# Decay matrices of the mLSTM: stabiliser rows by transposes of broadcast columns, the causal mask added by VectorE

## The chip, the cores and the metric

The kernel runs on one core of a Trainium2 chip. The metric is the device time of one execution in microseconds. A core has a tensor engine (PE, with its weight loads listed apart as PEld), a vector engine (DVE), a scalar engine (ACT), GpSimd (POOL) and SyncE (SP), which issues DMAs here. Each engine works through its own instruction queue in order and waits on semaphores for the others. TensorE writes to PSUM; VectorE and ScalarE read PSUM and SBUF.

## The reference, cut to what matters

The program is one step of a one-layer hybrid decoder: a half-step SwiGLU FFN, a mixer (mLSTM heads beside sliding-window attention heads, one input and one output projection), and a second half-step FFN, on a prompt of 1024 tokens and a batch of 8 x 4 sample tokens. The change lies in the mLSTM's chunk step:

```python
b = jnp.cumsum(jax.nn.log_sigmoid(fg), axis=-1)
causal = jnp.tril(jnp.ones((L, L), dtype=bool))
D = jnp.where(causal, b[..., :, None] - b[..., None, :] + ig[..., None, :], -jnp.inf)
inter = b + m[..., None]
m_t = jnp.maximum(inter, jnp.max(D, axis=-1))
W = jnp.exp(D - m_t[..., None])                 # the decay matrix
S = jnp.einsum('bhtd,bhsd->bhts', q, k) * W
num = a[..., None] * jnp.einsum('bhtk,bhkv->bhtv', q, C) + jnp.einsum('bhts,bhsv->bhtv', S, v)
```

With a_s = ig_s - b_s and M_t the running maximum, W is exp(a_s - M_t) for s <= t and 0 elsewhere. The kernel holds it transposed: s on the partitions, t along the row, four heads side by side. So a_s is a column (the bias of the exponential), -M_t is a row that has to stand on every partition, and the mask is a large negative number where s > t.

## The kernel before, in words

The prompt's mLSTM is cut into chunks 0 to 7 of 128 tokens; chunk 8 holds the 32 sample tokens. All projections are dense products in three single-precision passes (`mm3`, recorded at L163 as all products are); they fill nearly all of TensorE's queue. The work of the mLSTM, the attention and the gates is spawned as generator tasks of a planner (`Order`). The planner keeps a clock, `od.now`, which `pe()` (L157) advances for each product that is issued: 0.11 us for a transpose (`tr=True`, recorded at L160), for a plain fp32 product 4 x max(n, 64)/2400 us. When a task's due time comes, its next step is issued between two dense products. So the program's order on each engine is fixed at build time, and the planner's costs take part in it. The Tile layer then adds the waits.

`gates` (L1378) works on the four heads as 4 partitions: the row I holds -M_t at its end, and G the four groups of columns that the chunk step needs. One transpose of G per chunk (`gT`) and one VectorE copy give `K.cols[:, c]`: for each of the chunk's 128 tokens 4 groups x 4 heads. `gates_sample` (L1414) does the same for chunk 8.

`decay_matrix` (L1671) makes E = W for a chunk. In a PSUM bank named E (pool "a", two banks, shared with the scores S and the transposed keys tT) TensorE sums a product of a bf16 identity with the mask `maskb` (128 x 512) and four fp32 products of a one-hot column of the identity (4 partitions) with the rows H, which put -M_t on all partitions. ScalarE then takes four exponentials from PSUM to SBUF (L1682), each with its bias column. `scores` (L1685) makes S = k q on TensorE, and VectorE multiplies S into E (L1693). `state_keys` (L1697) transposes the keys (tT) and VectorE scales them (kw, L1705). `mlstm_state` then uses E (intra) and kw (U), `mlstm_norm` ends the chunk (hn, hT). `mlstm_sample` (L1802) calls `scores` for chunk 8 with slices of 32. The bf16 identity `identb` is made in `mix_setup` (L1294) from the fp32 one.

Around chunks 0 to 3 the dense work is the input projection (`po`, `pz`); around chunks 5 to 7 it is the rest of that and the output projection (`pw`), with the gating of the finished chunks (z, og, ul) on VectorE and ScalarE.

Of the kernel before, what the change touches and what calls it, by code (L numbers as in the profile page):

```python
# [9 lines left out]
F32 = mybir.dt.float32  # L10
F32R = mybir.dt.float32r
BF16 = mybir.dt.bfloat16
I32 = mybir.dt.int32
AF = mybir.ActivationFunctionType
ALU = mybir.AluOpType

P = 128
# [1231 lines left out]
HM = 4  # L1249
# [44 lines left out]
def mix_setup(K):  # L1294
    nc, A = K.nc, K.A
    mk = tmp(K, "mk", 162)
    nc.sync.dma_start(mk, A["c_mask"])
    K.maskb = K.cp.tile([P, 160], BF16, tag="maskb", name="maskb")
    nc.vector.tensor_copy(K.maskb, mk[:, 0:160])
    K.bmask = K.cp.tile([P, 2], F32, tag="bmask", name="bmask")  # L1300
    nc.vector.tensor_copy(K.bmask, mk[:, 160:162])
    K.identb = K.cp.tile([P, P], BF16, tag="identb", name="identb")
    nc.vector.tensor_copy(K.identb, K.ident)
    K.zero = K.cp.tile([P, 1], F32, tag="zero", name="zero")
    nc.vector.memset(K.zero, 0.0)
    K.bg = K.cp.tile([P, 8], F32, tag="bg", name="bg")
    nc.sync.dma_start(K.bg, A["b_gate"].to_broadcast([P, 8]))
    K.m0 = K.cp.tile([4, 8], F32, tag="m0", name="m0")
    nc.sync.dma_start(K.m0, A["state_mlstm_m"][0].rearrange("b h -> h b"))
    sk = K.cp.tile([8, 1], F32, tag="sk", name="sk")  # L1310
    nc.sync.dma_start(sk, A["attn_sinks"][0].rearrange("(h o) -> h o", o=1))
    ps = sbank(K, "sk")
    pe(K, ps[:, 0:8], sk.to_broadcast([8, P]), K.ident[0:8, 0:8], start=True, stop=True)
    oh = tmp(K, "oh", P)[0:8]
    nc.vector.tensor_copy(oh.rearrange("p (b h t) -> p b h t", b=4, h=8),
                          K.ident[0:8, 0:8].unsqueeze(1).unsqueeze(3).to_broadcast([8, 4, 8, 4]))
    pe(K, ps[:, 8:9], oh, sk, start=True, stop=True)
    K.sink = K.cp.tile([P, 9], F32, tag="sink", name="sink")
    nc.vector.tensor_copy(K.sink, ps[:, 0:9])
    K.cols = K.cp.tile([P, 9, 4, 4], F32, tag="cols", name="cols")  # L1320
    K.dec = K.cp.tile([P, 2, 4, 8], F32, tag="dec", name="dec")
    K.mst = K.cp.tile([4, 9], F32, tag="mst", name="mst")
    nc.vector.memset(K.mst[:, 0:1], 0.0)

    K.sz = K.cp.tile([P, 14, 32], F32, tag="sz", name="sz")
# [52 lines left out]
def gates(K, n):  # L1378

    nc = K.nc  # L1380
    I, lf = K.H[n]
    b, G = tmp2(K, "gb")[0:4], slot(K, "G")
    nc.gpsimd.memset(G, 0.0)
    chunks = [(c, loc(c)[1]) for c in range(4 * n, 4 * n + 4)]
    one = K.ones[0:4].to_broadcast([4, P])
    zero = K.zero[0:4].to_broadcast([4, P])
    a = G[0:4]
    for c, o in chunks:
        nc.vector.tensor_tensor_scan(b[:, o:o + P], one, lf[:, o:o + P], 0.0, ALU.mult, ALU.add)
    M, d = lf, b  # L1390
    p = lambda x: pair(x)[:, :, 0:2 * P]
    nc.vector.tensor_tensor(p(a), p(I), p(b), op=ALU.subtract)
    for c, o in chunks:
        nc.vector.tensor_tensor_scan(M[:, o:o + P], zero, a[:, o:o + P], K.mst[:, c:c + 1], ALU.add, ALU.max)
        nc.vector.tensor_tensor(K.mst[:, c + 1:c + 2], b[:, o + P - 1:o + P], M[:, o + P - 1:o + P], op=ALU.add)
    nc.vector.tensor_scalar(p(I), p(M), -1.0, None, op0=ALU.mult)
    nc.vector.tensor_tensor(p(d), p(b), p(M), op=ALU.add)
    yield 7.0
    nc.scalar.activation(p(G[64:68]), p(d), AF.Exp, scale=-1.0)
    for c, o in chunks:  # L1400
        nc.scalar.activation(G[32:36, o:o + P], M[:, o:o + P], AF.Exp, bias=K.mst[:, c:c + 1], scale=-1.0)
        nc.scalar.activation(G[96:100, o:o + P], a[:, o:o + P], AF.Exp, bias=I[:, o + P - 1:o + P])
    if n == 1:
        nc.sync.dma_start(K.O["p_m"][0, 0].rearrange("(h o) -> h o", o=1), K.mst[:, 8:9])
    yield 9.0
    dec_bcast(K, [G[32:36, o + P - 1:o + P] for c, o in chunks], 0, 4 * n)
    for c, o in chunks:
        ps = bank(K, "gT", "b")
        pe(K, ps[:, 0:100], G[0:100, o:o + P], K.ident[0:100, 0:100], tr=True)
        nc.vector.tensor_copy(K.cols[:, c], ps[:, 0:P].rearrange("p (y s) -> p y s", s=32)[:, :, 0:4])  # L1410
    K.od.done.add(("gates", n))


def gates_sample(K):  # L1414

    nc = K.nc
    I, b = K.H[2]
    M, w, d = [K.Hs[:, 64 + 32 * i:96 + 32 * i] for i in range(3)]
    G4 = tmp(K, "G", P)
    nc.gpsimd.memset(G4, 0.0)  # L1420
    G = G4[:, 0:32]
    a = G[0:4]
    v4 = lambda x: x.rearrange("p (b t) -> p b t", t=4)
    for s in range(1, 4):
        nc.vector.tensor_tensor(v4(b)[:, :, s], v4(b)[:, :, s], v4(b)[:, :, s - 1], op=ALU.add)
    nc.vector.tensor_tensor(a, I, b, op=ALU.subtract)
    for s in range(4):
        prev = K.m0 if s == 0 else v4(M)[:, :, s - 1]
        nc.vector.tensor_tensor(v4(M)[:, :, s], v4(a)[:, :, s], prev, op=ALU.max)
    nc.vector.tensor_tensor(d, b, M, op=ALU.add)  # L1430
    nc.scalar.activation(G[64:68], d, AF.Exp, scale=-1.0)
    nc.vector.tensor_tensor(v4(w), K.m0.unsqueeze(2).to_broadcast([4, 8, 4]), v4(M), op=ALU.subtract)
    nc.vector.tensor_tensor(v4(b), v4(a), v4(M)[:, :, 3:4].to_broadcast([4, 8, 4]), op=ALU.subtract)
    nc.vector.tensor_scalar(I, M, -1.0, None, op0=ALU.mult)
    nc.scalar.activation(G[32:36], w, AF.Exp)
    nc.scalar.activation(G[96:100], b, AF.Exp)
    mn = small(K, "mn", 8)[0:4]
    nc.vector.tensor_copy(mn, v4(d)[:, :, 3])
    nc.sync.dma_start(K.O["s_m"][0].rearrange("b h -> h b"), mn)
    yield 9.0  # L1440
    dec_bcast(K, [v4(G[32:36])[:, :, 3]], 1, 0)
    ps = bank(K, "gT", "b")
    nc.gpsimd.tensor_copy(G4[:, 32:P].rearrange("p (c t) -> p c t", c=3), G.unsqueeze(1).to_broadcast([P, 3, 32]))
    pe(K, ps[:, 0:100], G4[0:100], K.ident[0:100, 0:100], tr=True)
    nc.vector.tensor_copy(K.cols[:, 8], ps[:, 0:P].rearrange("p (y s) -> p y s", s=32)[:, :, 0:4])

    ps = bank(K, "scol", "b")
    for h in range(HM):
        pe(K, ps[32 * h:32 * h + 32, 0:4], G[0:100], K.ident[0:100, h::32],
           start=True, stop=True, tile_position=(0, 32 * h))  # L1450
    K.scc = K.cp.tile([P, 4], F32, tag="scc", name="scc")
    nc.vector.tensor_copy(K.scc, ps[:, 0:4])
    K.od.done.add(("gates", 2))
# [214 lines left out]
    return r  # L1668


def decay_matrix(K, H, c, w, home):  # L1671

    nc = K.nc
    ps = bank(K, "E", "a")
    mask = K.maskb[:, 0:P] if w == P else K.maskb[0:32, P:160]
    pe(K, ps[0:w, 0:4 * w].rearrange("p (h t) -> p h t", h=4), K.identb[0:w, 0:w],
       mask.unsqueeze(1).to_broadcast([w, 4, w]), start=True, stop=False)
    for h in range(HM):
        pe(K, ps[0:w, h * w:(h + 1) * w], K.ident[0:4, h:h + 1].to_broadcast([4, w]), H, start=False, stop=(h == HM - 1))
    E = home(K, "E")[:, 0:4 * w]  # L1680
    for h in range(HM):
        nc.scalar.activation(E[0:w, h * w:(h + 1) * w], ps[0:w, h * w:(h + 1) * w], AF.Exp,  # L1682
                             bias=K.cols[0:w, c, 0, h:h + 1])
    return E


def scores(K, c, k, q, H, w, home):

    E = decay_matrix(K, H, c, w, home)
    S = bank(K, "S", "a")  # L1690
    for h in range(HM):
        pe(K, S[0:w, h * w:(h + 1) * w], k[h], q[h], start=True, stop=True)
    K.nc.vector.tensor_tensor(E[0:w], S[0:w, 0:4 * w], E[0:w], op=ALU.mult)  # L1693
    return E

# [15 lines left out]
def chunk_scores(K, c):  # L1711
    n, o = loc(c)
    k = [K.k[h][n][:, o:o + P] for h in range(HM)]
    E = scores(K, c, k, [K.q[h][n][:, o:o + P] for h in range(HM)], K.H[n][0][:, o:o + P], P, tmp)
    return E, state_keys(K, k, [K.cols[:, c, 3, :]], tmp)[0]


# [84 lines left out]
def mlstm_sample(K):  # L1802

    nc, A, O = K.nc, K.A, K.O
    c = 8
# [10 lines left out]
    ps = bank(K, "n0T", "c")  # L1816
# [2 lines left out]
    nc.vector.tensor_copy(n0.rearrange("p b h -> p (b h)"), ps[:, 0:32])  # L1819
    for b in range(8):  # L1820
        state(b)
    E = scores(K, c, [K.sz[:, 6 + h] for h in range(HM)], [K.sz[:, 10 + h] for h in range(HM)], K.H[2][0], 32, slot)

    kr = slot(K, "kr")[:, 0:512]
    nc.gpsimd.tensor_copy(kr.rearrange("p (h c t) -> p h c t", h=4, c=4),
# [9 lines left out]
    for hp in range(2):  # L1835
        q = slot(K, "qm")[:, 0:512]
# [7 lines left out]
    for b0 in range(0, 8, 2):  # L1844
# [3 lines left out]
        for b, Cb in zip(bs, C):  # L1848
            for h in range(HM):
                q = qm[h // 2][:, (h % 2) * 256 + b * 32:(h % 2) * 256 + b * 32 + 32]  # L1850
                pe(K, pi[32 * h:32 * h + 32, 0:129], q, Cb[:, h], start=(b == 0), stop=(b == 7),
                   tile_position=(0, 32 * h))
        for hp in range(2):
            pu = [bank(K, "sU", "ba"[hp]) for b in bs]
            for x in range(2):
                h = 2 * hp + x
# [4 lines left out]
            for b, ps, Cb in zip(bs, pu, C):  # L1861
                for x in range(2):
                    h = 2 * hp + x
# [325 lines left out]
```

## Time and profile before

| | |
|---|---|
| median of three runs | 1987.2 us (1985.57 to 1987.73) |
| the profiled execution's own time | 1986.58 us |
| its span | 1984.8 us |
| TensorE busy | 1956.4 us, 99% |
| VectorE busy | 1229.6 us, 62% |
| ScalarE busy | 901.6 us, 45% |
| granted TensorE clock, mean | 0.999 of full speed |

The span is the time from the first to the last recorded instruction of the profiled execution; its own time is 1.8 us above. Busy shares are means over the whole span; the mLSTM's chunks lie between about 1007 and 1150 us of it. In a timeline a group of like instructions stands in one row with the start of the first and the time to the end of the last; matmuls overlap, so the step from one row's start to the next one's tells what a group takes of the engine.

### The profile page before, as it was taken

What the parts mean: (1) busy time and instruction counts of PE and PEld (TensorE: products, weight loads), DVE (VectorE), ACT (ScalarE), POOL (GpSimd) and SP (SyncE); (2) the same over time, 40 slices, a digit from 0 to 9 for tenths busy, and PEclk for the clock granted to TensorE, in tenths of its full rate; (3) what the DMA queues carried; (4) which work ended last, traced back from release to release, by engine and by line L of the source; (5) the groups of instructions that cost most, each with busy time, mean ns of one, the idle gap of its engine ahead of it and who ended that gap; (6) DMA issues with size and microseconds to landing.
All of it is one profiled execution on the core that took longest, in us unless ns stands there. A gap on an engine that the chain in (4) does not pass through costs nothing.

```text
span 1984.8 us, 40434 instructions
## 1 busy us (share of the span) xinstructions
PE 1956.4 (99%) x16012; PEld 1915.5 (97%) x16012; DVE 1229.6 (62%) x2945; ACT 901.6 (45%) x2169; POOL 39.8 (2%) x191
## 2 busy tenths in 40 slices
PE   7999999999999999999999999999999999999998
PEld 7999999999999999987999999999999999999998
DVE  7756555557568436467546757885555555856764
ACT  6533333336456332346243655453333334645554
POOL 1000000000000002100101000000000000000000
PEclk9999999999999999999999999999999999999999
DMA  7223322236357352201224234323222322746684
GB/s 234 71 76 100 105 79 76 76 98 197 106 158 236 104 136 97 69 1 38 79 65 120 74 112 131 121 77 96 76 87 86 98 76 84 214 123 205 196 256 128
DMA packets 283582, 226.42 MB, mean 114 GB/s; under 512 B 22440, under 2 KB 256032, under 8 KB 283392
## 3 DMA queue, kind: packets, MB, share of 16 engines
q1 hardware_dynamic: 283392, 223.84, 37.3%
q8 instruction: 125, 2.05, 0.4%
q14 instruction: 65, 0.53, 0.1%
HBM read 175.70 MB, written 47.89 MB: 113 GB/s over the span
## 4 chain that ended last, share of the span: by engine, by line
PE 91%; DMA 3%; DVE 3%; ACT 2%; issue 0%; SPq 0%; DVEq 0%; ACTq 0%
PE gu L163 40%; PE pd L163 23%; PE pz L163 7%; PE pw L163 5%; PE pl L163 3%; PE pv L163 2%; PE po L163 2%; DMA raw<-ffn_w_down 1%; ACT sws L1505 1%; PE cs L163 1%; DMA hq<-h 1%; PE swo L163 1%; PE E L163 1%; PE yT L160 1%; PE sws L163 1%; PE S L163 0%
## 5 line engine op out<-in xcount | busy, mean ns | idle before, releaser
L163 PE MATMUL gu<-Xh,wh 128*128 128x264 f32 x2240 | 636.4, 284 | 0.9 <-ACT sc L1006 0.8
L163 PE MATMUL gu<-Xl,wh 128*128 128x264 f32 x2240 | 636.8, 284 | 0.0
L163 PE MATMUL gu<-Xh,wl 128*128 128x264 f32 x2240 | 635.5, 284 | 0.0
L163 PE MATMUL pd<-hq,wh 128*128 128x264 f32 x2752 | 509.0, 286 | 1.5 <-ACT sc L1110 1.3
L163 PEld LDWEIGHTS pd<-hq,wh 128*128 128x128 f32 x2752 | 426.4, 188 | 2.7 <-ACT sc L1110 2.2
L163 PEld LDWEIGHTS gu<-Xh,wh 128*128 128x128 f32 x2240 | 421.3, 188 | 1.5 <-ACT sc L1006 1.5
L163 PEld LDWEIGHTS gu<-Xh,wl 128*128 128x128 f32 x2240 | 421.6, 188 | 0.0
L163 PEld LDWEIGHTS gu<-Xl,wh 128*128 128x128 f32 x2240 | 421.2, 188 | 0.0
L207 DVE TENSOR_TENSOR wl<-raw,wh 128x512 fp32r<-128x512 f32 (+1 forms) x442 | 288.5, 666 | 173.3 <-ACT wh L206 159.1
L163 PE MATMUL pd<-hq,wl 128*128 128x264 f32 x1376 | 391.5, 285 | 0.3 <-DVE wl L207 0.2
L206 ACT CAST wh<-raw 128x512 fp32r<-128x512 f32 (+1 forms) x442 | 259.4, 601 | 249.0 <-PE pd L163 112.7
L163 PEld LDWEIGHTS pd<-hq,wl 128*128 128x128 f32 x1376 | 258.8, 188 | 1.0 <-DVE wl L207 0.9
L1006 ACT COPY sc<-gu 128x264 f32<-128x264 f32 x240 | 91.0, 380 | 353.9 <-PE gu L163 333.6
L207 DVE TENSOR_TENSOR wl<-ws,wh 128x512 fp32r<-128x512 f32 x192 | 130.5, 689 | 94.0 <-ACT wh L206 90.7
L1017 DVE TENSOR_TENSOR h<-gu,sc 128x264 f32<-128x264 f32 x120 | 51.8, 432 | 136.8 <-PE gu L163 85.9
L206 ACT CAST wh<-ws 128x512 fp32r<-128x512 f32 x192 | 115.0, 622 | 8.3 <-DVE ws L783 7.9
L1023 DVE TENSOR_TENSOR sc<-gu,sc 128x264 f32<-128x264 f32 x120 | 51.8, 431 | 94.8 <-PE gu L163 47.1
L163 PE MATMUL pz<-xh,wh 128*128 128x264 f32 x352 | 102.1, 290 | 0.0
L163 PE MATMUL pz<-xh,wl 128*128 128x264 f32 x352 | 101.0, 287 | 0.0
L163 PE MATMUL pz<-xl,wh 128*128 128x264 f32 x352 | 100.7, 286 | 0.0
L1018 ACT ACTIVATE h<-h 128x264 f32<-128x264 f32 x120 | 51.0, 425 | 108.2 <-DVE h L1017 108.2
L206 ACT CAST hq<-hq 128x264 fp32r<-128x264 f32 x192 | 70.8, 412 | 22.3 <-DMA hq<-h 17.3
(413 smaller groups left out, 3027.3 us busy)
## 6 DMA issues: line engine op xcount, KB each, us to landing
raw<-ffn_w_down SPq DMA_DIRECT2D x64, 512.0 KB
h<-h SPq DMA_DIRECT2D x84, 264.0 KB
raw<-ffn_w_gate SPq DMA_DIRECT2D x42, 512.0 KB
raw<-ffn_w_up SPq DMA_DIRECT2D x42, 512.0 KB
hq<-h SPq DMA_DIRECT2D x160, 132.0 KB
raw<-ffn_w_down SPq DMA_DIRECT2D x40, 384.0 KB
x<-xs SPq DMA_DIRECT2D x48, 264.0 KB
raw<-w_in SPq DMA_DIRECT2D x21, 512.0 KB
```

The source lines that it names most:

```text
L160: K.nc.tensor.transpose(out, lhsT, rhs)
L163: ins = K.nc.tensor.matmul(out, lhsT, rhs, start=start, stop=stop, **kw)
L206: K.nc.scalar.copy(hi, src)
L207: (eng or K.nc.vector).tensor_tensor(lo, src, hi.bitcast(F32), op=ALU.subtract)
L1006: nc.scalar.copy(sc[n][:, g], ps)
L1017: nc.vector.tensor_tensor(d, bk[tg, g], sc[n][:, g], op=ALU.add)
L1018: nc.scalar.activation(d, d, AF.Silu)
L1023: nc.vector.tensor_tensor(sc[n][:, g], src, sc[n][:, g], op=ALU.add)
L1505: nc.scalar.activation(s, s, AF.Exp, bias=nmx[:, y:y + 1], accum_out=den[:, y:y + 1])
```

## The change

The rows -M_t no longer reach the partitions by products with one-hot columns. `gates` transposes the four rows I to four more columns of `K.cols` (a fifth group, copied together with the others: 20 values a row instead of 16; for the sample chunk by a copy of its own). `decay_matrix` takes the column of a head, broadcasts it along the row, and transposes that [w, w] tile into PSUM: four transposes. VectorE adds the mask to all four heads on the way from PSUM to SBUF, and the exponentials work in place in SBUF. `identb` is gone, and `scores` no longer gets H. Lines below L1303 move by up to two or four: the exponential stands at L1684, the mask's addition at L1681, the multiplication at L1695, kw at L1707.

```diff
--- before.py
+++ after.py
@@ -1299,8 +1299,6 @@
     nc.vector.tensor_copy(K.maskb, mk[:, 0:160])
     K.bmask = K.cp.tile([P, 2], F32, tag="bmask", name="bmask")
     nc.vector.tensor_copy(K.bmask, mk[:, 160:162])
-    K.identb = K.cp.tile([P, P], BF16, tag="identb", name="identb")
-    nc.vector.tensor_copy(K.identb, K.ident)
     K.zero = K.cp.tile([P, 1], F32, tag="zero", name="zero")
     nc.vector.memset(K.zero, 0.0)
     K.bg = K.cp.tile([P, 8], F32, tag="bg", name="bg")
@@ -1317,7 +1315,7 @@
     pe(K, ps[:, 8:9], oh, sk, start=True, stop=True)
     K.sink = K.cp.tile([P, 9], F32, tag="sink", name="sink")
     nc.vector.tensor_copy(K.sink, ps[:, 0:9])
-    K.cols = K.cp.tile([P, 9, 4, 4], F32, tag="cols", name="cols")
+    K.cols = K.cp.tile([P, 9, 5, 4], F32, tag="cols", name="cols")
     K.dec = K.cp.tile([P, 2, 4, 8], F32, tag="dec", name="dec")
     K.mst = K.cp.tile([4, 9], F32, tag="mst", name="mst")
     nc.vector.memset(K.mst[:, 0:1], 0.0)
@@ -1407,7 +1405,8 @@
     for c, o in chunks:
         ps = bank(K, "gT", "b")
         pe(K, ps[:, 0:100], G[0:100, o:o + P], K.ident[0:100, 0:100], tr=True)
-        nc.vector.tensor_copy(K.cols[:, c], ps[:, 0:P].rearrange("p (y s) -> p y s", s=32)[:, :, 0:4])
+        pe(K, ps[:, P:P + 4], I[:, o:o + P], K.ident[0:4, 0:4], tr=True)
+        nc.vector.tensor_copy(K.cols[:, c], ps[:, 0:160].rearrange("p (y s) -> p y s", s=32)[:, :, 0:4])
     K.od.done.add(("gates", n))
 
 
@@ -1442,7 +1441,9 @@
     ps = bank(K, "gT", "b")
     nc.gpsimd.tensor_copy(G4[:, 32:P].rearrange("p (c t) -> p c t", c=3), G.unsqueeze(1).to_broadcast([P, 3, 32]))
     pe(K, ps[:, 0:100], G4[0:100], K.ident[0:100, 0:100], tr=True)
-    nc.vector.tensor_copy(K.cols[:, 8], ps[:, 0:P].rearrange("p (y s) -> p y s", s=32)[:, :, 0:4])
+    pe(K, ps[0:32, P:P + 4], I, K.ident[0:4, 0:4], tr=True)
+    nc.vector.tensor_copy(K.cols[:, 8, 0:4], ps[:, 0:P].rearrange("p (y s) -> p y s", s=32)[:, :, 0:4])
+    nc.vector.tensor_copy(K.cols[0:32, 8, 4], ps[0:32, P:P + 4])
 
     ps = bank(K, "scol", "b")
     for h in range(HM):
@@ -1668,25 +1669,26 @@
     return r
 
 
-def decay_matrix(K, H, c, w, home):
+def decay_matrix(K, c, w, home):
 
     nc = K.nc
     ps = bank(K, "E", "a")
     mask = K.maskb[:, 0:P] if w == P else K.maskb[0:32, P:160]
-    pe(K, ps[0:w, 0:4 * w].rearrange("p (h t) -> p h t", h=4), K.identb[0:w, 0:w],
-       mask.unsqueeze(1).to_broadcast([w, 4, w]), start=True, stop=False)
     for h in range(HM):
-        pe(K, ps[0:w, h * w:(h + 1) * w], K.ident[0:4, h:h + 1].to_broadcast([4, w]), H, start=False, stop=(h == HM - 1))
+        pe(K, ps[0:w, h * w:(h + 1) * w], K.cols[0:w, c, 4, h:h + 1].to_broadcast([w, w]), K.ident[0:w, 0:w], tr=True)
     E = home(K, "E")[:, 0:4 * w]
+    v = lambda t: t[0:w, 0:4 * w].rearrange("p (h t) -> p h t", h=4)
+    nc.vector.tensor_tensor(v(E), v(ps), mask.unsqueeze(1).to_broadcast([w, 4, w]), op=ALU.add)
     for h in range(HM):
-        nc.scalar.activation(E[0:w, h * w:(h + 1) * w], ps[0:w, h * w:(h + 1) * w], AF.Exp,
+        e = E[0:w, h * w:(h + 1) * w]
+        nc.scalar.activation(e, e, AF.Exp,
                              bias=K.cols[0:w, c, 0, h:h + 1])
     return E
 
 
-def scores(K, c, k, q, H, w, home):
-
-    E = decay_matrix(K, H, c, w, home)
+def scores(K, c, k, q, w, home):
+
+    E = decay_matrix(K, c, w, home)
     S = bank(K, "S", "a")
     for h in range(HM):
         pe(K, S[0:w, h * w:(h + 1) * w], k[h], q[h], start=True, stop=True)
@@ -1711,7 +1713,7 @@
 def chunk_scores(K, c):
     n, o = loc(c)
     k = [K.k[h][n][:, o:o + P] for h in range(HM)]
-    E = scores(K, c, k, [K.q[h][n][:, o:o + P] for h in range(HM)], K.H[n][0][:, o:o + P], P, tmp)
+    E = scores(K, c, k, [K.q[h][n][:, o:o + P] for h in range(HM)], P, tmp)
     return E, state_keys(K, k, [K.cols[:, c, 3, :]], tmp)[0]
 
 
@@ -1819,7 +1821,7 @@
     nc.vector.tensor_copy(n0.rearrange("p b h -> p (b h)"), ps[:, 0:32])
     for b in range(8):
         state(b)
-    E = scores(K, c, [K.sz[:, 6 + h] for h in range(HM)], [K.sz[:, 10 + h] for h in range(HM)], K.H[2][0], 32, slot)
+    E = scores(K, c, [K.sz[:, 6 + h] for h in range(HM)], [K.sz[:, 10 + h] for h in range(HM)], 32, slot)
 
     kr = slot(K, "kr")[:, 0:512]
     nc.gpsimd.tensor_copy(kr.rearrange("p (h c t) -> p h c t", h=4, c=4),
```

The order of instructions changes in three places that matter here. On TensorE, the first chunk's decay matrix and scores; E, S and tT are the PSUM tiles named above, `xh`, `xl`, `wh`, `wl` belong to the dense projection `po`. Before:

```order
L163 LDWEIGHTS identb
L163 MATMUL E_12981<-maskb,identb 128x512
L163 MATMUL E_12981<-H_11845,ident 128x128 x4
L163 MATMUL S_12992<-z_12741,z_11720 128x128
L163 MATMUL S_12992<-z_12806,z_12096 128x128
L163 MATMUL S_12992<-z_12871,z_12378 128x128
L163 MATMUL S_12992<-z_12936,z_12605 128x128
L163 MATMUL po_12977<-xh_1304_8187,wh_12773 128x264
L163 MATMUL po_12977<-xl_1305_8188,wh_12773 128x264
L163 MATMUL po_12977<-xh_1304_8187,wl_12774 128x264
L160 MATMUL tT_12998<-ident,z_11720 128x128
```

And with the change:

```order
L160 MATMUL E_12989<-ident,cols 128x128 x4
L163 MATMUL S_13000<-z_12749,z_11718 128x128
L163 MATMUL S_13000<-z_12814,z_12136 128x128
L163 MATMUL S_13000<-z_12879,z_12423 128x128
L163 MATMUL S_13000<-z_12944,z_12611 128x128
L163 MATMUL po_12985<-xh_1304_8185,wh_12781 128x264
L163 MATMUL po_12985<-xl_1305_8186,wh_12781 128x264
L160 MATMUL tT_13006<-ident,z_11718 128x128
```

Four transposes stand where the mask's product and the four one-hot products stood; one dense product fewer stands between the scores and the keys' transposes.

On VectorE, the first two chunks, with the tail of the projection's work (z, wl) ahead of them. Before:

```order
L2062 TENSOR_TENSOR z_12936<-pz_12939,rrow_8675 128x264
L207 TENSOR_TENSOR wl_12973<-raw_12966,wh_12972 128x512
L1693 TENSOR_TENSOR E_12987<-S_12992,E_12987 128x512
L1705 TENSOR_TENSOR kw_13003<-tT_12998,cols 128x512
L1693 TENSOR_TENSOR E_13011<-S_13016,E_13011 128x512
L1705 TENSOR_TENSOR kw_13027<-tT_13022,cols 128x512
```

With the change:

```order
L2064 TENSOR_TENSOR z_12944<-pz_12947,rrow_8673 128x264
L207 TENSOR_TENSOR wl_12981<-raw_12974,wh_12980 128x512
L1681 TENSOR_TENSOR E_12994<-E_12989,maskb 128x512
L1707 TENSOR_TENSOR kw_13011<-tT_13006,cols 128x512
L1695 TENSOR_TENSOR E_12994<-S_13000,E_12994 128x512
L1681 TENSOR_TENSOR E_13018<-E_13013,maskb 128x512
L1707 TENSOR_TENSOR kw_13035<-tT_13030,cols 128x512
L1695 TENSOR_TENSOR E_13018<-S_13024,E_13018 128x512
```

Each chunk has an addition more, and the keys' scaling now stands ahead of the multiplication by S instead of behind it.

On VectorE again, chunks 4 and 5, behind the gate of the output (og). Before:

```order
L2100 TENSOR_TENSOR og_14078<-po_14079,rrow_10023 128x264
L1693 TENSOR_TENSOR E_14146<-S_14151,E_14146 128x512
L1705 TENSOR_TENSOR kw_14162<-tT_14157,cols 128x512
L207 TENSOR_TENSOR wl_14358<-raw_14353,wh_14357 128x512
L1693 TENSOR_TENSOR E_14170<-S_14175,E_14170 128x512
L1705 TENSOR_TENSOR kw_14186<-tT_14181,cols 128x512
```

With the change:

```order
L2102 TENSOR_TENSOR og_14086<-po_14087,rrow_10021 128x264
L1681 TENSOR_TENSOR E_14158<-E_14153,maskb 128x512
L1707 TENSOR_TENSOR kw_14175<-tT_14170,cols 128x512
L1681 TENSOR_TENSOR E_14182<-E_14177,maskb 128x512
L1695 TENSOR_TENSOR E_14158<-S_14164,E_14158 128x512
L207 TENSOR_TENSOR wl_14352<-raw_14347,wh_14351 128x512
L1707 TENSOR_TENSOR kw_14199<-tT_14194,cols 128x512
L1695 TENSOR_TENSOR E_14182<-S_14188,E_14182 128x512
```

Here the addition of chunk 5 stands ahead of the multiplication of chunk 4, so that this one waits for TensorE's transposes of chunk 5.

## Rows read from the trace of the kernel before

**Rows 1.** The page's first lines: span, and each engine's busy time, share, instructions
```profile
span 1984.8 us, 40434 instructions
PE 1956.4 (99%) x16012; PEld 1915.5 (97%) x16012; DVE 1229.6 (62%) x2945; ACT 901.6 (45%) x2169; POOL 39.8 (2%) x191
```

**Rows 2.** TensorE's waits after 1000 us: for whom; total us, times, longest
```profile
PE sU L163 <- DVE kw L1705: 0.8, 1, 0.8
...
PE pd L163 <- DVE wl L207: 0.2, 1, 0.2
```

**Rows 3.** Windows: length, busy PE, PEld, DVE, ACT, POOL; clock, DMA share, GB/s
```profile
1005.00:1030.00 25.00, 24.97 (x197) 23.14 (x196) 13.63 (x43) 11.34 (x32) 0.38 (x2) 1.00 0.13 36
...
1105.00:1145.00 40.00, 39.99 (x319) 37.93 (x318) 33.42 (x112) 30.54 (x99) 0.00 (x0) 1.00 0.14 41
```

**Rows 4.** Timeline of TensorE, first chunk: start us, us, what
```profile
1007.66 0.39 PE L163 MATMUL E<-maskb,identb 128*128 128x512 bf16 x1
1007.98 1.15 PE L163 MATMUL E<-H,ident 4*128 4x128 f32 x8
1009.07 1.16 PE L163 MATMUL S<-z,z 128*128 128x128 f32 x8
...
1010.43 0.60 PE L160 MATMUL tT<-ident,z 128*128 128x128 f32 x4
1010.79 0.37 PE L163 MATMUL po<-xh,wh 128*128 128x264 f32 x1
```

**Rows 5.** Timeline of the sample chunk's decay matrix on TensorE
```profile
1079.42 0.22 PE L163 MATMUL E<-maskb,identb 32*32 32x128 bf16 x1
1079.48 0.41 PE L163 MATMUL E<-Hs,ident 4*32 4x32 f32 x8
1079.82 0.44 PE L163 MATMUL S<-sz 128*32 128x32 f32 x8
```

**Rows 6.** Timeline of TensorE, transposes of broadcast columns at 1914 us
```profile
1914.58 0.49 PE L160 MATMUL rb<-ident,r 128*128 128x128 f32 x3
1914.83 0.49 PE L163 MATMUL pd<-hq,wh 128*128 128x264 f32 x2
```

**Rows 7.** Tile tT: ns of one, least, median, most
```profile
L160 PE MATMUL tT<-ident,z x32: 270/272/273, 1010.4 to 1128.7; 128*128 128x128 f32 x32
```

**Rows 8.** Timeline of TensorE, products with four columns out
```profile
982.61 0.24 PE L163 MATMUL scol<-ident,G 100*32 100x4 f32 x8
982.79 0.39 PE L163 MATMUL pz<-xh,wh 128*128 128x264 f32 x1
```

**Rows 9.** Tiles E and num on VectorE and ScalarE: ns, as above
```profile
L1682 ACT ACTIVATE E<-E,cols x36: 263/368/382, 1009.2 to 1127.0; 128x128 f32<-128x128 f32 x32, 32x32 f32<-32x32 f32 x4
L1693 DVE TENSOR_TENSOR E<-S,E x9: 281/691/692, 1010.4 to 1128.2; 128x512 f32<-128x512 f32 x8, 32x128 f32<-32x128 f32 x1
...
L1663 ACT ACTIVATE hn<-num x32: 296/308/342, 1020.6 to 1147.8; 128x128 f32<-128x128 f32 x32
L1764 DVE TENSOR_TENSOR hn<-num,r x8: 681/692/695, 1027.6 to 1151.2; 128x512 f32<-128x512 f32 x8
```

**Rows 10.** Timelines of ScalarE and VectorE, first chunk; in brackets idle, releaser
```profile
1009.17 1.14 ACT L1682 ACTIVATE E<-E,cols 128x128 f32<-128x128 f32 x4 [1.17 <-PE E L163]
1010.35 0.69 DVE L1693 TENSOR_TENSOR E<-S,E 128x512 f32<-128x512 f32 x1 [1.61 <-ACT E L1682]
```

**Rows 11.** Timeline of VectorE, the longest work among chunks 5 to 7
```profile
1114.51 2.12 DVE L2043 SCALAR_TENSOR_TENSOR z<-z,gain,og 128x528 f32<-128x528 f32 x3
```

**Rows 12.** Start of the program: VectorE, then TensorE's first transposes
```profile
9.51 0.21 DVE L1303 CAST identb<-ident 128x128 bf16<-128x128 f32 x1
9.64 0.19 DVE L101 COPY gain<-gps 128x52 f32<-128x52 f32 x1
...
9.89 1.06 PE L160 MATMUL xsT<-ident,xt 32*128 32x32 f32 x8 [6.83 <-DVE gain L101]
```

**Rows 13.** Chain of waits, 0 to 40 us: the weights' first transfer
```profile
30.41 7.14 DMA raw<-ffn_w_gate
```

## The prediction

> **What bounds the kernel now.** I read the page's first lines, then TensorE's waits, then windows over the mLSTM, then the timelines of single chunks. TensorE is busy for 1956.4 of 1984.8 us [rows 1]. After 1000 us, which takes in all chunks, it waits five times in all: the longest is 0.8 us for kw of the sample tokens, the shortest shown 0.2 us [rows 2]. [...] So here the time is the sum of what TensorE issues, and each product taken from it counts in full until it waits for someone. VectorE has room around chunks 0 and 1 (13.63 of 25 us busy), and little where chunks 5 to 7 meet the output projection (33.42 of 40) [rows 3]. That is where the change can be paid for.
>
> **What goes from TensorE.** In a timeline the step from one row's start to the next is what a group takes. In the first chunk the mask's product starts at 1007.66, the four one-hot products (eight matmuls, two passes each) at 1007.98, the scores at 1009.07 [rows 4]: 0.32 for the mask, 1.09 for the rows, 1.41 us together. Eight chunks: 11.28. The sample chunk: 1079.42 to 1079.82, 0.40 [rows 5]. Removed: 11.68 us.
>
> **What comes to TensorE.** Four fp32 transposes of [128, 128] per chunk. The same kind stands behind the scores: the keys' four tT run from 1010.43 to the next product's start at 1010.79, 0.36 us for four [rows 4]. At 1914 us three transposes of just such broadcast columns (rb) take 1914.58 to 1914.83, 0.083 each, 0.33 for four [rows 6]. The upper bound is four whole durations, 4 x 0.272 = 1.09 [rows 7], if nothing overlapped. I take 0.36, of the same shape, number and place: 8 x 0.36 = 2.88. For the sample's four of 32 columns I take the pace of its one-hot matmuls, eight in 0.34 (1079.48 to 1079.82) [rows 5]: 0.17. The gates gain nine small transposes (4 x 128 to 128 x 4). Eight matmuls with four columns out take 0.18 us, 0.02 each [rows 8]; a whole duration is 0.27. I take 0.083, the step of a transpose, so 0.75. Added: 2.88 + 0.17 + 0.75 = 3.80, net 7.88 us gained before any wait.
>
> The rows show tT transposes of 272 ns that start 0.09 apart [rows 4, 7]. [...]
>
> **What comes to VectorE and ScalarE.** Per chunk one addition 128 x 512, PSUM and SBUF in, SBUF out. The multiplication by S is the same form and takes 691 ns (281 on the sample); hn, from SBUF alone, takes 692 [rows 9]. I take 0.69 from both sides: 8 x 0.69 + 0.28 = 5.80 us more for VectorE. Around chunks 0 to 3 its idle time hides that. In the dense window two of them raise 33.42 to 34.8 us, while the window shrinks by two nets of about one us to 38: 91% busy. The exponentials now read SBUF. From PSUM they take 368 ns; a Square 128x128 from SBUF takes 308 [rows 9]. I cost the difference at nothing, bound by 36 x 0.06 = 2.2 us either way, off TensorE's path. The gates' copies grow from 16 to 20 values a row and one small copy is added: nothing, hidden behind dense products, since no chunk starts until long after.
>
> The rows show a read from SBUF of this size as no longer than one from PSUM [rows 9]. [...]
>
> **What waits.** The chain of a chunk's E was: one-hot products, exponentials (1.14 us), multiplication [rows 10]. It becomes transposes, addition, exponentials, multiplication: 0.69 longer on VectorE and ScalarE, while the transposes end about 1.05 us sooner. VectorE sat idle 1.61 us before its multiplication, ScalarE 1.17 before its exponentials [rows 10], so an early chunk can bear this. Also the bank that E holds in pool "a" comes free after the addition now and not after the last exponential. Nothing is saved in waits: none of the five named E or S.
>
> Three instants look exposed, where TensorE needs something that stands behind an addition on VectorE: the banks of the second chunk (E and S need the two banks back, freed by the first chunk's addition, keys' scaling and multiplication, now in another order); chunk 5, whose scores need the bank that chunk 4's multiplication frees, and that multiplication stands behind chunk 5's addition, with a wl of the dense weights queued behind it; and chunk 7 or its neighbours in the dense window, where an addition stands behind or ahead of work like the three z of 2.12 us [rows 11], while transposes of hn and keys wait for VectorE's next result. The trace of before shows no such wait. Bounds: nothing, if the queues have slack everywhere; 5.80, if every addition is exposed. I price each of the three at one addition: 3 x 0.69 = 2.07.
>
> **The start.** The cast to the bf16 identity (0.21 us at 9.51) stands before the copy `gain`, which TensorE had waited 6.83 us for [rows 12]. That copy starts 0.13 us after the cast. I count it at nothing, because the chain at 30.41 runs into a weight transfer of 7.14 us [rows 13], which an earlier start of TensorE does not advance; bound: 0.13 gained.
>
> **The sum.** 1986.58 - 7.88 + 2.07 = 1980.77 for the profiled execution. The median of the runs shown is 0.62 above that execution, so 1981.4 us.
>
> **Rivals.**
>
> B, every addition is exposed. VectorE has no slack where chunks run beside other work, and TensorE waits each time: 1986.58 - 7.88 + 5.80 + 0.62 = 1985.1. For it: 91% in the dense window. Against: 13.63 of 25 us in the first [rows 3], and idle stretches of 1.61 us right before the multiplication [rows 10].
>
> C, slower: VectorE's queue becomes the bound of the dense stretch. In chunks 4 to 7 TensorE's transposes and banks wait for an addition that is itself queued behind long gating work, priced as the 2.12 us of z [rows 11] and 0.69: 4 x 2.81 = 11.24; chunks 0 to 3 pay 4 x 0.69 = 2.76, the sample 0.28. 1986.58 - 7.88 + 14.28 + 0.62 = 1993.6. It ends slower than before once waits exceed 7.88 us, about 1.0 per chunk. For it: 33.42 of 40 us is a mean with full stretches in it. Against: TensorE has dense products queued between a chunk's steps, and hardly waits at that load now [rows 2].
>
> D, transposes do not overlap. Each of the 45 holds TensorE for its 0.272 us: 12.24 against 11.68 removed, 1986.58 + 0.56 + 2.07 + 0.62 = 1989.8. It loses from a step of (11.68 - 2.07) / 45 = 0.21 us. For it: nothing but the duration [rows 7]. Against: 0.083 and 0.09 in two places [rows 4, 6]. [...]
>
> **How the numbers follow.** The forecast holds for waits from nothing to about 3.9 us: with the least transposes (0.33 per chunk, 0.02 each in the gates) and 0.13 at the start, 1978.4; with 3.9, 1983.2. Chance 0.70. B 0.17, C 0.07, D 0.06. For all cases I go from 1977.8 (0.6 under the least, the distance of median and profiled execution) to 1986.0 (B and half the spread of the runs); outside lie C, D and a remainder. A measurement of this kernel can tell about 0.2% from no change, 4 us: faster is below 1983.2, slower above 1991.2. Faster is the forecast, 0.70; within the bound are B and D, 0.23; slower is C, 0.07.
>
> **What would show it.** In the changed profile: E's four transposes from their start to the scores' start about 0.36 us (D: 1.1); E on VectorE at L1681 nine times, 0.69 each; TensorE's waits after 1000 us with new entries for E, S, tT or hT against VectorE of about 2 us in all (B: near 6, in most chunks; C: above 8, in chunks 4 to 7); PE's busy time about 8 us lower and the span some 6. The prediction is wrong if the scores or the keys wait in the early chunks too, if the exponentials from SBUF take clearly over 0.37 us, or if the mLSTM's window shortens by less than a chunk's 1.05 us a chunk without a wait that shows it.

## The result, and the profile after

The changed kernel takes 1991.99 us (median of 20, 1985.68 to 1996.94), the kernel before 1987.7 us beside it (20 runs): ratio 1.0021 with a 95% interval of 1.0014 to 1.0029. It is slower by about 4 us, where it was forecast to be faster, at 1981.4 us. Its profiled execution took 1990.92 us with a mean granted clock of 0.996; that of before had 0.999.

The first lines of the page, and TensorE's waits after 1000 us (for whom, total us, times, longest):

```profile
span 1989.1 us, 40357 instructions
PE 1957.8 (98%) x15976; PEld 1917.7 (96%) x15976; DVE 1235.0 (62%) x2954; ACT 902.8 (45%) x2169; POOL 41.1 (2%) x191
```

```profile
PE gu L163 <- ACT sc L1006: 1.5, 1, 1.5
PE pd L163 <- ACT sc L1110: 1.0, 1, 1.0
PE sU L163 <- DVE kw L1707: 0.8, 1, 0.8
PE cs L163 <- ACT sq L693: 0.5, 1, 0.5
PE cs L163 <- DVE sq L596: 0.4, 1, 0.4
PE yT L160 <- DVE yo L1239: 0.2, 1, 0.2
```

Beside [rows 1, 2]: VectorE has 5.4 us more to do (5.80 had been worked out), and TensorE has not one wait on E, S, tT or hT. What is new are the two waits for sc in the second FFN (before had 0.2 us there). TensorE's busy time is 1.4 us higher, where about 8 us less was forecast. The decay matrix of the first chunk and of the sample chunk on TensorE (start, us, what), to be read beside [rows 4, 5]:

```profile
1014.33 0.60 PE L160 MATMUL E<-ident,cols 128*128 128x128 f32 x4
1014.76 1.06 PE L163 MATMUL S<-z,z 128*128 128x128 f32 x8
...
1082.20 0.28 PE L160 MATMUL E<-ident,cols 32*32 32x32 f32 x4
1082.41 0.44 PE L163 MATMUL S<-sz 128*32 128x32 f32 x8
```

0.43 us in place of 1.41, and 0.21 in place of 0.40: the transposes overlap (one lasts 0.27 us). The gates' transposes, between those of G:

```profile
941.25 0.31 PE L160 MATMUL gT<-ident,G 100*128 100x100 f32 x1
941.49 0.22 PE L160 MATMUL gT<-ident,H 4*128 4x4 f32 x1
941.64 0.30 PE L160 MATMUL gT<-ident,G 100*128 100x100 f32 x1
```

This one takes 0.15 us (941.49 to 941.64), and so do most of the nine; one took 0.09 and the sample's 0.10. On VectorE and ScalarE, tile E (ns least, median, most), beside [rows 9]:

```profile
L1684 ACT ACTIVATE E<-E,cols x36: 304/387/406, 1016.0 to 1133.0; 128x128 f32<-128x128 f32 x32, 32x32 f32<-32x32 f32 x4
L1681 DVE TENSOR_TENSOR E<-E,maskb x9: 272/691/692, 1015.3 to 1130.5; 128x512 f32<-128x512 f32 x8, 32x128 f32<-32x128 f32 x1
```

So TensorE got the work that was forecast, and nobody keeps it waiting there. The windows show what did happen (length, busy PE, PEld, DVE, ACT, POOL, then granted clock, DMA share, GB/s):

```profile
964.00:968.00 4.00, 4.00 (x24) 3.10 (x25) 0.89 (x5) 0.41 (x2) 0.00 (x0) 0.95 0.56 168
968.00:972.00 4.00, 4.00 (x20) 3.87 (x20) 2.37 (x20) 0.00 (x0) 0.19 (x1) 0.50 0.22 53
972.00:976.00 4.00, 4.00 (x37) 3.70 (x37) 1.46 (x9) 1.52 (x3) 0.00 (x0) 0.69 0.28 78
1088.00:1092.00 4.00, 4.00 (x52) 2.82 (x49) 4.00 (x13) 0.00 (x0) 0.80 (x2) 1.00 0.76 163
1092.00:1094.00 2.00, 2.00 (x13) 1.63 (x13) 1.67 (x8) 0.00 (x0) 0.19 (x1) 0.98 0.53 164
1094.00:1097.00 3.00, 3.00 (x26) 2.39 (x25) 0.30 (x2) 0.62 (x1) 0.19 (x1) 0.50 0.58 175
1097.00:1100.00 3.00, 3.00 (x33) 2.83 (x30) 1.68 (x7) 0.62 (x1) 0.00 (x0) 0.95 0.03 8
```

Twice, besides the program's last microseconds, TensorE's clock falls to 0.50, where before had 1.00 in every window from 0 to 1900 us. Its windows over the sample chunk:

```profile
1080.00:1090.00 10.00, 9.22 (x112) 8.18 (x109) 7.82 (x22) 3.90 (x10) 4.17 (x17) 1.00 0.99 252
1090.00:1100.00 10.00, 10.00 (x115) 8.68 (x114) 7.42 (x25) 4.91 (x8) 1.13 (x6) 1.00 0.70 206
```

Busy time does not betray a fall: PE is busy for 4.00 of 4.00 us from 968 to 972 and for 3.00 of 3.00 from 1094 to 1097. What the engine does around the second fall is in its timeline:

```profile
1086.82 1.49 PE L163 MATMUL sU<-vs,kw 32*128 32x129 f32 x16 [0.78 <-DVE kw L1707]
1088.24 0.65 PE L163 MATMUL sinter<-Cb,qm 128*32 128x129 f32 x16
...
1089.96 0.71 PE L163 MATMUL sU<-vs,kw 32*128 32x129 f32 x4
1090.59 0.39 PE L163 MATMUL po<-xh,wh 128*128 128x264 f32 x1
1090.91 0.71 PE L163 MATMUL sU<-vs,kw 32*128 32x129 f32 x4
1091.55 0.39 PE L163 MATMUL po<-xl,wh 128*128 128x264 f32 x1
...
1094.14 0.42 PE L163 MATMUL po<-xl,wh 128*128 128x264 f32 x1
1094.36 0.42 PE L163 MATMUL po<-xh,wl 128*128 128x264 f32 x1
```

The sample chunk's state products (sU, on 32 rows) begin with a block of sixteen; from 1090.0 to 1093.6 they come four at a time with one or two dense products between them. Then the dense product's step is 0.22 us (1094.14 to 1094.36) and not 0.12 (1099.21 to 1099.33, the clock at 1.00 again). In the kernel before the same 32 products stood together, done within 4 us, with 15 dense ones behind them:

```profile
1084.23 0.71 PE L163 MATMUL sU<-vs,kw 32*128 32x129 f32 x8 [0.78 <-DVE kw L1705]
1084.88 0.65 PE L163 MATMUL sinter<-Cb,qm 128*32 128x129 f32 x16
1085.45 0.71 PE L163 MATMUL sU<-vs,kw 32*128 32x129 f32 x8
1086.10 0.65 PE L163 MATMUL sinter<-Cb,qm 128*32 128x129 f32 x16
1086.67 1.57 PE L163 MATMUL sU<-vs,kw 32*128 32x129 f32 x16
1088.17 0.39 PE L163 MATMUL po<-xh,wh 128*128 128x264 f32 x1
...
1090.18 0.65 PE L163 MATMUL sinter<-Cb,qm 128*32 128x129 f32 x16
```

The order of the program, which nobody meant to change here, is another.

Each execution comes with a mean granted clock (to 0.001, so that one execution's loss is known to 1 us). Span times one minus it, averaged over executions, is my estimate of the loss to the clock: a fall to 0.50 counts with half its length (the dense product's steps of 0.22 and 0.12 us are near that). The time less that loss I call the rest. Before: loss 4.4 +- 0.2 us (standard error), rest 1983.4 +- 0.2 (the 110 executions beside the experiments). The changed kernel: loss 9.9 +- 0.6, rest 1982.2 +- 0.3 (33, two of the experiments included).

### The profile page after: what moved, and what is told of

It is laid out like the page before. It is cut to its first block, busy times and chain, and to the rows that moved or that the text cites. A ratio compares the mean times of both kernels' runs of the same rounds, so it can differ in the third digit from the quotient of the medians.

```text
span 1989.1 us, 40357 instructions
## 1 busy us (share of the span) xinstructions
PE 1957.8 (98%) x15976; PEld 1917.7 (96%) x15976; DVE 1235.0 (62%) x2954; ACT 902.8 (45%) x2169; POOL 41.1 (2%) x191
## 4 chain that ended last, share of the span: by engine, by line
PE 91%; DVE 3%; DMA 3%; ACT 2%; issue 0%; SPq 0%; DVEq 0%; ACTq 0%
PE gu L163 40%; PE pd L163 24%; PE pz L163 7%; PE pw L163 5%; PE pl L163 3%; PE po L163 2%; PE pv L163 2%; DMA raw<-ffn_w_down 1%; PE cs L163 1%; ACT sws L1506 1%; PE sws L163 1%; PE swo L163 1%; PE yT L160 1%; DVE sws L1494 0%; DMA hq<-ht 0%
```

## The experiments

The ratio is to the executions of before that ran beside each. Theory A says that the shifted order makes the clock fall, theory B that the small transposes do; theory S, from e9 on, is A with the sample chunk as the place.

| | runs | median | ratio to before, 95% | loss to the clock | rest |
|---|---|---|---|---|---|
| e1 changed kernel again | 12 | 1993.65 | 1.0016 (1.0002 to 1.0030) | 9.1 +- 1.2 | 1982.7 |
| e2 old plan | 11 | 1986.59 | 0.9986 (0.9977 to 0.9995) | 5.4 +- 0.5 | 1981.1 |
| e3 no small transposes | 11 | 1987.58 | 0.9996 (0.9986 to 1.0006) | 6.3 +- 0.8 | 1981.7 |
| e4 gates' part alone | 11 | 1991.25 | 1.0012 (1.0003 to 1.0020) | 6.5 +- 0.5 | 1984.9 |
| e5 before, new plan | 12 | 1991.06 | 1.0016 (1.0004 to 1.0028) | 6.8 +- 1.0 | 1984.4 |
| e6 gates in old order | 11 | 1990.56 | 1.0017 (1.0006 to 1.0029) | 10.7 +- 1.1 | 1980.8 |
| e7 chunks on old plan | 11 | 1985.96 | 0.9988 (0.9979 to 0.9998) | 7.2 +- 0.5 | 1978.5 |
| e8 DMA and old plan | 11 | 1985.52 | 0.9989 (0.9977 to 1.0001) | 7.0 +- 1.0 | 1978.6 |
| e9 sample's order | 12 | 1984.53 | 0.9990 (0.9980 to 0.9999) | 5.8 +- 0.5 | 1978.7 |
| e10 sample spread | 12 | 1985.19 | 0.9993 (0.9984 to 1.0002) | 5.5 +- 0.3 | 1979.6 |
| e13 sample's order on e6 | 12 | 1985.94 | 0.9991 (0.9982 to 1.0000) | 6.4 +- 0.4 | 1979.4 |

The executions of before beside them: loss 4.7 and rest 1984.0 (e1 to e4), 4.4 and 1983.4 (e5 to e8), 3.8 and 1982.8 (e9, e10), 4.6 and 1983.2 (e13). Rests of different groups so compare to about 1 us only.

**e1**, unaltered. 

> The changed kernel once more, unaltered. Theory (clock): its profile shows TensorE's granted clock at half in two stretches, 967.8 to 974.2 us and 1093.8 to 1097.6 us, which cost half their length, 3.2 and 1.9 us; the kernel before has none there. If these falls belong to the program, a second profile shows them at the same two places and the time stays near 1992 (4 us above before). Rival (chance waits): the loss lies in the FFNs, where TensorE waited 4.8 us for sc in the changed kernel's profile and 2.1 in that of before; then those waits change from profile to profile, and the falls are by-play that comes and goes.

The sample's fall came again, at 1097 to 1101 us, behind the same products, which ran 4 us later; others stood between 620 and 640, 940 and 950, 970 and 980, 1270 and 1290 (mean clock of this profile 0.994). Five of the twelve executions took 1986.6 to 1987.5 us at 0.997 or 0.998, seven 1993.4 to 1997.9 at 0.993 to 0.995: time goes with the clock. The FFN waits were there again (2.3 us after 1290), so the clock and the rival, waits, both keep a part, the clock the larger.

**e2.**
```diff
     # decay_matrix, behind the four transposes
+    K.od.now += 4 * w / 2400 + 4 * 4 * max(w, 64) / 2400 - 4 * 0.11
     # gates and gates_sample, behind each small transpose
+        K.od.now -= 0.11
```


> The changed kernel, but the planner's clock is advanced for the decay matrix as it was before (1.07 us a chunk in place of 0.44) and not at all for the nine transposes in the gates. The order around the gates is then that of before, with the small transposes put in between. Theory A (the shifted order makes the clock fall): the fall at 968 goes, about 1988.8, and the one at 1094 goes too if the sample's order comes back, about 1987. Theory B (the small transposes themselves make it fall): the fall at 968 stays, 1990 to 1992. Rival (no part of the clock): 1992.

Not an instruction less, and 5 us faster than the changed kernel: loss 5.4 in place of 9.9. This is for theory A, though not in every point: there was no fall around the gates, but one of 3.5 us in the sample, whose products are back in blocks but for two dense ones, and one near 1700 (steps of 0.22 us from 1700.53 on).

**e3.**
```diff
     # cut: the wider rows of cols and its other readers
+    nc.sync.dma_start(p(G[4:8]), p(I))     # gates, before yield 7.0; the sample alike
-        pe(K, ps[:, P:P + 4], I[:, o:o + P], K.ident[0:4, 0:4], tr=True)
+        nc.vector.tensor_copy(K.cols[:, c], ps[:, 0:P]...[:, :, 0:8])
```


> The changed kernel without the nine small transposes: a DMA puts the rows beside the four of G that are transposed anyway, and the one copy takes eight columns of each group. Theory B: 9 x 0.15 us and the fall at 968 (3.2) go: 1987.4, with the fall at 1094 still there. Theory A: only if the order goes back does the fall go; 1990.6 otherwise. Rival (a DMA of a few rows arrives late and the gates' transposes wait for it): above 1992.

Median as theory B said, with falls of the clock at 920 to 940 and 1270 (0.997 over the profile); by its profile the sample, in the changed kernel's broken order, did not fall (dense steps of 0.12 us behind the groups of four, 1091.25 to 1091.37). Ten of the eleven executions had a mean clock of 0.996 to 0.998, one 0.993. That is against theory S and is taken up by e14.

**e4.**
```diff
+        pe(K, ps[:, P:P + 4], I[:, o:o + P], K.ident[0:4, 0:4], tr=True)   # in before.py
         # cut: the wider copy, and the same for the sample
```


> The kernel before, with only the gates' part of the change: nine small transposes and the wider copy, their columns unused; the decay matrix as before. Theory B: 9 x 0.15 = 1.4 us and a fall of 3.2 on top of before, 1992.3. Without a fall 1989.1. Rival (the loss comes from the decay matrix's part): within 1 us of before plus 1.4, and no fall.

The rest rises by 1.0 us against the executions beside it and by 1.5 against all of before, near nine times 0.15; the loss rises by 2, and there is no fall at 968 in the profile (mean clock 0.998). Theory B explains less than half of the 5.5 us lost to the clock.

**e5.**
```diff
+    K.od.now -= 4 * w / 2400 + 4 * 4 * max(w, 64) / 2400 - 4 * 0.11   # decay_matrix of before.py
+        K.od.now += 0.11                                             # gates, behind each gT
```


> The kernel before, none of its instructions changed, but the planner's clock is advanced as the changed kernel advances it (0.44 us for a decay matrix in place of 1.07, and 0.11 more for each of the nine transposes of the gates). So the order alone shifts. Theory A (the shifted order lets TensorE's clock fall): the mean loss to the clock, span times one minus the mean clock, rises from 4.7 us (35 executions of before) towards the 9 to 10 of the changed kernel, and the time to about 1992. Theory B (the small transposes are needed for it): the loss stays at 4 to 6.5, the time within 1 us of before.

The kernel before becomes 3.5 us slower by two numbers of its planner alone: loss 6.8 and rest +1. That is half of what theory A wanted; the interval of the ratio allows 0.8 to 5.6 us.

**e6** and **e7** are halves of e2: the gates' lines alone, and the decay matrix's line alone. 

> The changed kernel, with only the nine small transposes left out of the planner's clock: the order around the gates is that of before, the order in the chunks that of the changed kernel. Theory A with the gates as the place: the fall at 968 is gone and the loss is 6 to 7 us, 1988.5. Theory A with the chunks as the place: loss near 9, 1992, fall at 1094.

> The changed kernel, with the planner's clock advanced for the decay matrix as before: new order around the gates, old plan in the chunks. Gates as the place: falls at 940 or 968, loss 8 to 9, 1990.5. Chunks as the place: loss 5 to 6, 1987.

For the larger part the place is the chunks. With the gates in their old order the loss stays (10.7; the clock at 0.50 from 1085 to 1095 us); with the old plan in the chunks it goes down to 7.2, more than the 5 to 6 expected, and a fall around 968 is still in that profile (0.50 from 968.3 to 973.3).

**e8**, e3 with e2's line in `decay_matrix`. 

> A version put together from the two best so far: rows brought beside G by a DMA in place of the nine small transposes, and the old planner's cost of the decay matrix. Time with the clock's loss taken off: 1981.1 of the old-plan version less 9 x 0.13 = 1.2, 1979.9; with a loss of 5.4 as there 1985.3, 3 us under before. If the loss is more like that of the version with the DMA alone (6.3), 1986.2.

As fast as forecast, in part by luck: the loss is 7.0 where 5.4 was put in, the rest 1978.6 where 1979.9 was. The rest is 4.8 us under before.

**e9.**
```diff
     # mlstm_sample, behind scores(...)
+    K.od.now += 0.4
     kr = slot(K, "kr")[:, 0:512]
```


> The changed kernel with one line more: the planner's clock goes 0.4 us ahead in the sample chunk, behind its scores. The order up to there, gates and chunks 0 to 3, is the changed kernel's; the sample's state products (sU) come in blocks as in the kernel before, no longer four at a time between single dense products. Theory S (that broken run of small products is where the clock falls at 1094): no fall there, the mean loss to the clock goes from 9.8 to 6 or 7 us, 1988 to 1989. Rival (falls come at any weak place by chance, and the sample is one of many): loss stays at 9 to 10, 1991 to 1992.

One line, and the changed kernel is faster by 7.5 us by the medians, 6 by the ratios to before, and 2 under before. Of that 4.1 us are the clock; that the rest fell too, from 1982.2 to 1978.7, theory S had not forecast (1988 to 1989). TensorE's timeline at the sample and the window over it:

```profile
1086.13 0.71 PE L163 MATMUL sU<-vs,kw 32*128 32x129 f32 x8 [0.78 <-DVE kw L1707]
1086.78 0.65 PE L163 MATMUL sinter<-Cb,qm 128*32 128x129 f32 x16
1087.35 0.71 PE L163 MATMUL sU<-vs,kw 32*128 32x129 f32 x8
1088.00 0.65 PE L163 MATMUL sinter<-Cb,qm 128*32 128x129 f32 x16
1088.58 0.71 PE L163 MATMUL sU<-vs,kw 32*128 32x129 f32 x8
```

```profile
1083.00:1109.00 26.00, 24.97 (x271) 22.07 (x270) 19.64 (x55) 11.15 (x25) 5.07 (x22) 1.00 0.62 171
```

Blocks again, though the last has two dense products in it, and the clock stays at 1.00. Around 970 it falls in this profile too (0.70 from 967.6 to 972.7), so the gates' fall and the sample's are two things.

**e10**, e8 with `K.od.now -= 0.8` at that place. 

> The version with the DMA and the old planner's cost (1985.5), with the planner's clock set back 0.8 us in the sample chunk: its state products then stand in three even blocks with 9 and 15 dense products between them. Theory S: no fall in the sample, the loss goes from 7.0 to about 5, 1983.6. Rival (chance): as the version without the line, 1985.5.

No fall in the sample (1.00 from 1078 to 1106), loss 5.5, near theory S; but the rest is a microsecond worse than e8's, so the time is the rival's.

**e11** and **e12** are further profiles of both kernels, unaltered. 

> The changed kernel unaltered, a third profile, to see at which places its clock falls: both theories say again near 968 and 1094, if these are the program's own weak places; others mean chance.

> The kernel before, unaltered, a second profile: its mean loss of 4.4 to 4.7 us is 2.7 at the end of the program and about one fall elsewhere in every second execution. Expected: no fall between 930 and 1110.

Before fell once, at 620 to 630 (0.83 over these 10 us). The changed kernel fell in the sample from 1083.7 to 1100.7, 17 us that count as a loss of 8.5 (the window covers them):

```profile
1083.00:1100.00 17.00, 17.00 (x109) 13.62 (x106) 8.84 (x29) 1.53 (x3) 1.54 (x6) 0.52 0.35 93
```

TensorE's timeline where that fall begins:

```profile
1083.44 0.39 PE L163 MATMUL po<-xh,wh 128*128 128x264 f32 x1
1083.67 0.32 PE L163 MATMUL po<-xl,wh 128*128 128x264 f32 x1
1083.80 0.41 PE L163 MATMUL po<-xh,wl 128*128 128x264 f32 x1
1084.14 1.09 PE L163 MATMUL sinter<-Cb,qm 128*32 128x129 f32 x16
1085.15 1.23 PE L163 MATMUL sU<-vs,kw 32*128 32x129 f32 x4
```

The clock is down before the first group of four sU, behind the block of sixteen. It is so in e6, e14 and e15 too (down by 1083.4 to 1084.9, the first four at 1085.0 to 1086.3). Only in the changed kernel's profile above and in e1 does the fall come at the end of the groups of four. So those groups cannot be what starts the long falls.

The changed kernel did not fall near 968 here (1.00 from 955 to 985). So the sample looks like a weak place of this order, the gates like one of several where falls come and go.

**e13**, e9's line on e6, to see whether it helped by chance. 

> The kernel with the gates' old order (loss to the clock 10.7 us, 1990.6), with the one line in the sample chunk that moves the planner's clock 0.4 us ahead, so that its state products come in blocks again. Theory S: loss of about 6, no fall in the sample, 1985. Rival (the line helped e9 by chance, by shifting all that follows): loss stays at 9 to 11, 1990.

Loss from 10.7 to 6.4, no fall in the sample (its profile falls around 968 instead, 0.50 from 967.6 to 972.6): it repeats.

**e14**, **e15** (e3 again) and **e16** (e5 again). 

> The version with the DMA in place of the small transposes (e3), a second profile. Its sample chunk has the changed kernel's broken order. If that order alone makes the fall: a fall between 1080 and 1105 in at least one of two more profiles. [...]

> As the run before this one, a third profile of the same kernel.

> The kernel before with the shifted plan (e5), a second profile: its sample's products are broken up nearly as in the changed kernel. A fall between 1080 and 1110 if that order alone makes it; none if it takes more.

Both further profiles of e3 fall in the sample; the first of them:

```profile
1080.00:1090.00 10.00, 9.22 (x71) 6.70 (x69) 7.11 (x20) 1.14 (x3) 2.01 (x8) 0.67 0.72 175
1090.00:1100.00 10.00, 10.00 (x60) 8.65 (x61) 4.17 (x14) 1.67 (x3) 0.75 (x4) 0.50 0.27 80
```

The two executions had a mean clock of 0.993 and 0.994, where ten of e3's eleven had 0.996 to 0.998; e3 and these ran at different times, on different chips, and which of the two matters was not tried. e16 does not fall in the sample (1.00 from 1078 to 1110); its sample is broken up a little less, in blocks of 14, 2, 8, 4 and 4. In all, profiles with the changed kernel's order in the sample fall there in six of seven (the changed kernel three times, e6, e14, e15; not the first of e3), profiles with blocks in one of nine (e2). The falls of the six cost 1.8 us (twice), 5.3 (e6) and 8.4 (three times). Six of the same seven, all but the changed kernel's first, also fall for some 3.5 us between 1270 and 1282 (0.66 over 5 us in e6, e11, e14 and e15), and of the eleven other profiles one does (e8, at 1266, 0.69 over 5 us). An edit in the sample moves all that follows as well, so these runs do not tell whether that fall hangs on the sample's order or on the shift. Why one order falls and another does not, and why e5's is spared, they do not say either.

## Why the prediction was wrong

**The step that failed** is the first: "So here the time is the sum of what TensorE issues, and each product taken from it counts in full until it waits for someone." The clock was taken as given from the trace of before (1.00 in both windows of [rows 3]), and not one rival had it. The changed kernel loses 9.9 us to it, before 4.4: 5.5 us, the sign of the result. In the six profiles with its sample's order that fell there, the sample chunk alone cost 1.8 to 8.4 us of clock. The transposes as such are not the cause there: e9 and e13 have them all and do not fall in the sample. The shift comes from the planner: a decay matrix advances its clock by 4 x 0.11 = 0.44 us where it had been 0.21 + 4 x 0.21 = 1.07, so tasks fall due at other dense products, and the sample chunk's state products came in another order. The order was read at the places where E stands, and not over those state products, which the change does not touch. That the planner's clock in the chunks moves the loss is shown by e6 and e7, that the sample's order does by e9 and e13; what in that order makes the clock fall stays open, and e3, which has it and lost only 6.3 us, shows that it does not always.

The trace shows what a fall does: a dense product's step is 0.22 us at 0.50 (1094.14 to 1094.36) and 0.12 at 1.00 (1099.21 to 1099.33), with PE listed as busy for 4.00 of 4.00 us at 1.00 (1088 to 1092) and for 3.00 of 3.00 at 0.50 (1094 to 1097); so the profile's busy share does not foretell it.

**Removed work**: right by the steps. 8 x (1.41 - 0.43) + 0.40 - 0.21 = 8.03 us off the decay matrices, 8.63 forecast; four transposes took 0.43 and not 0.36, the sample's four 0.21 and not 0.17. **Small transposes**: mis-sized, 0.15 for most in place of 0.083, at most 1.35 us for nine and not 0.75. **Waits**: forecast 2.07, none at the three instants; the additions took 0.69 us as said and VectorE bore them (34.28 of 40 us at 1105 to 1145, 33.42 before). Rivals B and C fall with that, D with the step of the transposes; that the measured time lies near C's 1993.6 is chance, since the waits that C is made of are not there. **Exponentials** from SBUF: 387 ns against 368, 19 more, off the path; the sample's 32x32, the least in both rows, 304 against 263, 41 more. They were costed at nothing, and at 36 x 0.06 us at most, which holds.

**The sum** without the clock: 8.03 - 1.35 = 6.7 us by the steps, 5.81 forecast. Against the executions of before beside each, the rest shows 4.9, 4.8 and 4.0 us in e7, e8 and e9, 2.3 to 3.7 in e2, e3, e6, e10 and e13, and only 1.2 to 1.3 in the changed kernel. Sections of the profiles tell why in part. Up to the gates' end (scol) the changed kernel's three profiles, less the clock, are 0.5 to 3.3 us later than before's two, 2.2 on the mean, of which the small transposes explain 1.35 at most. From there to the second FFN's first gu they are 5.0 to 6.0 us shorter, where the steps say 8.03, e9's 5.9. From there to the output's transposes the three are 1.7 to 2.7 us longer, and e9 has no more than before. The new waits for sc stand there (2.2 to 2.5 us; 0.2 and 1.3 in before's two profiles). They come where a burst of reloads starts; in all profiles with the new decay matrix eight loads in SP's queue take 4.5 to 5.0 us there, 3.7 in all others. That is not the whole reason, since e9 has the slow loads (4.6) without the longer section. Why is open, and it was not tried.

## What to carry to other kernels

Where a planner's costs set the order, a cheaper operation moves everything behind it: compare the order over the whole stretch up to where it is the same again, not where the change stands. On a kernel that TensorE bounds, read the granted clock over several executions, first where many small products stand together (here the sample chunk: the changed kernel's order fell there in six profiles of seven); which order keeps the clock was found here by trying, not by a rule. One profile of before at 1.00 does not mean that the clock stays there: its second profile has 0.83 from 620 to 630 us. A version with one line more (e9) keeps a part of the gain: 0.9990 of before (0.9980 to 0.9999), where the changed kernel has 1.0021.

## What had not been expected of the hardware

The clock falls in before too, in one of two profiles at 620 to 630 us (0.83), after TensorE had waited 1.6 us at the end of the first FFN; over 110 executions it loses 4.4 us, 2.5 to 2.7 of them, in its two profiles, in the program's last microseconds. A fall lasted from 3.5 to 17 us. With equal instructions the twelve executions of e1 lay in two groups, 1986.6 to 1987.5 us at a mean clock of 0.997 or 0.998 and 1993.4 to 1997.9 at 0.993 to 0.995; the twenty of the first measurement fill the space between.
